# Last FFN of a hybrid encoder block: the last column group in two quads of seven block products, two weight sums of each by accumulating transfers

## Chip, cores and metric

The kernel runs on one core of one Trainium2 chip. The metric is device time in microseconds (us) of one execution; lower is better. A core has a tensor engine (PE; its weight loads are listed as PEld), a vector engine (DVE), a scalar engine (ACT), a GpSimd engine (POOL) and a sync engine (SP). In this kernel SP issues the plain weight loads, and POOL issues the few transfers that add to what lies in SBUF.

## What is computed

The reference is one residual block on `x` (256 tokens, width 2048): a SwiGLU feed-forward half step, a mixer of mLSTM heads and a gated linear recurrence, and a second SwiGLU half step. Only the last one matters here:

```python
def _swiglu(u, w13, w2):
    g, v = jnp.split(u @ w13, 2, axis=-1)
    return (jax.nn.silu(g) * v) @ w2
...
        y = _swiglu(modulate(x, 2), ffn2_w13[l], ffn2_w2[l])
        x = _layer_norm(ALPHA * x + FFN_WEIGHT * gate[:, 2, None, :] * y, ln_g[l, 2], ln_b[l, 2])
```

`w13` is 2048 x 11264 (gate half and value half of 5632 columns each), `w2` is 5632 x 2048, all in float32.

## The kernel before

**Precision.** The tensor engine multiplies in fp32r. Each float32 weight tile is split into a high part (a cast on ACT, name `h...`) and a low part (a subtraction raw minus high on DVE, name `l...`); activations are split in the same way. A product of a weight block (512 rows x 512 columns, one 1 MB tile of 128 x 2048) with 128 tokens is 12 matmuls of 128x512: for each of four row blocks high x high, low weight x high, high weight x low, in this order (`mov_t`). So the first matmul of a product needs the high part and the second needs the low part.

**Tiling of the last FFN (`last_ffn`, L1167).** The 5632 hidden columns go in 11 groups b = 0 to 10 of 512. A group needs eight weight tiles of `w13`, four row quarters of the gate columns (tiles 0 to 3) and four of the value columns (4 to 7), for two token halves t = 0, 1. Done plainly, that is 16 products. `fast_group` (L1361) does it with fewer. A *quad* q is the 2 x 2 x 2 problem made of two row quarters (2q, 2q+1), the gate and value columns, and the two token halves; with a = tile 2q, b = 2q+1, c = 4+2q, d = 5+2q it takes seven products in place of eight, each with its own weight tile:

- P1 uses a. P5 uses c - a, which DVE writes over a. P6 uses a - c - d, which DVE writes over the same place. P3 uses d, P2 uses b.
- P7 uses c + d, written over c; P4 uses a - c - d + b, written over a once more.

The two last sums are made either by DVE or, in the groups listed in `SUMMED` (L48), by a transfer that POOL issues and that adds the tile from HBM to what stands in SBUF (`onto`, L1219). The place a is thus written and read in a row: loaded, split for P1, summed, split for P5, summed, split for P6, summed, split for P4.

The first token sums that P5, P6, P3 and P7 multiply are in `ws[0]` (for quad 0) and `ws[1]` (for quad 1), made once.

**Single and double groups.** A single group has quad 0 in seven products and the other two row quarters in plain products: G (gate columns) and V (value columns), two tiles each, 24 matmuls a tile. A double group (listed in `DOUBLE`, L45) has both quads in seven products. Groups 2, 4, 6 and 8 are double, 1, 3, 5, 7, 9 and 10 are single. The order of the products on PE is written out by hand in a string for each kind (S2, S4, S10, D6, L56 to L59): P1 to P7, G and V are products, X is a tile of the second matrix `w2` (24 matmuls, for the group before), and t turns a finished group of hidden values (four 128x128 transposes).

**Order on the other engines.** All work of this stage is first recorded as steps (`Plan`, L95). PE's steps keep the order of the strings. The planner gives each step of DVE, ACT, POOL and SP a due time from PE's steps that need it, and by its own costs and the buffers that come free it settles the order on each engine and the buffer that each tile takes. Every engine's queue then runs strictly in that order, each instruction waiting for what it needs.

**After group 10.** `gated` (L1573) prepares two `w2` tiles into the space of the activations; seven `w2` tiles follow (`end_tile`), then the last column tile and the final layer norm.

**Names in the profile.** `rfw` is a raw `w13` tile, `hfw_100P` / `lfw_100P` the high and low parts of the products of group 10, quad 0 (`101P` quad 1), `100G`, `101V` and so on the plain ones, `f` the accumulators and partial sums of a group, `th`/`ht` the turned hidden values, `lw`/`hw` a `w2` tile, `tl` its accumulators, `yacc` the residual. Nearly all instructions of this stage carry L359, the helper that records them.

Of the kernel before, what the change touches and what calls it, by code (L numbers as in the profile page):

```python
# [41 lines left out]

SLOT = 2176

DOUBLE = (2, 4, 6, 8)  # L45
HOLD = ("slot", "row")
BY_DMA = ("P2", "P3")
SUMMED = (1, 2, 3, 4, 5, 6, 7, 8, 9)  # L48
TURNED = ()
SOONER = True  # L50
ANY = ("raw", "lo", "slot", "row", "hi")
# [3 lines left out]

S4 = "P1 t X t P5 X P6 P3 X P7 P2 G P4 G X V V"  # L56
S2 = "P1 t G t P5 G P6 P3 P7 V P2 P4 V"
S10 = "P1 t G t P5 X P6 P3 P2 P4 G X P7 V V"
D6 = "P1 t X t P5 P6 X P3 P7 X P2 P4 X P1 X P5 P6 X P3 P7 X P2 P4 X"  # L59


# [33 lines left out]
class Plan:  # L95
# [14 lines left out]
    def place(self, tag, make, ap=None):  # L110
        tags = (tag,) if isinstance(tag, str) else tag
        p = Place(tags, (lambda _: make()) if isinstance(tag, str) else make, ap)
        if ap is not None and tags:
            p.tag, p.asked = tags[0], True
            self.taken[p.tag] += 1
        return p
# [166 lines left out]
def block_kernel(ctx: ExitStack, tc: tile.TileContext, a: dict, out: bass.AP):  # L283
# [80 lines left out]
    V, A, G, T, Q = (Pinned(e) for e in (nc.vector, nc.scalar, nc.gpsimd, nc.tensor, nc.sync))  # L364
# [146 lines left out]
    def mov_t(ps, hl, acth, actl, k0, t, first, last, pe=nc.tensor, **kw):  # L511

        hi, lo = hl
        tk = slice(t * P, (t + 1) * P)
        for j in range(4):
            w = slice(j * 512, (j + 1) * 512)
            o = like(ps, hi)
            pe.matmul(o, acth[:, k0 + j, tk], cut(hi, w), start=first and j == 0, stop=False, **kw)  # L518
            pe.matmul(o, acth[:, k0 + j, tk], cut(lo, w), start=False, stop=False, **kw)  # L519
            end = pe.matmul(o, actl[:, k0 + j, tk], cut(hi, w), start=False, stop=last and j == 3, **kw)  # L520
        return end
# [30 lines left out]
    def rows(k):  # L552

        return lambda: [u2[:, i:i + 4].rearrange("p a w b -> p (a w b)") for i in (k, k + 4)]
# [612 lines left out]
    def last_ffn(s, w13, w2):  # L1167
        n_b = NFF // 4
        sts = new_stats(s)
        plan = Plan({"raw": 4, "hi": 3, "lo": 3, "row": 2, "slot": 6, "ps": 8, "u": 2, "gy": 2, "x": 1})  # L1170
# [29 lines left out]
        def bank_place(name):  # L1200
            return place("ps", lambda: bank(name))
# [4 lines left out]
        def load(src, name, to=None):  # L1206
            p = to or raw_place(name)
            op("Q", 0.4, lambda: Q.dma_start(p(), src), writes=[p], moves=1.0)
            return p

        def split(p, name, into=None, by=None):
            hi = into[0] if into else any_place("h" + name, F32R, HIGH)
            lo = into[1] if into else any_place("l" + name, F32R, LOW)
            op("A", 1.82, lambda: A.copy(hi(), like(p(), hi())), reads=[p], writes=[hi], seq=None if into else "hi", by=by)
            op("V", 2.21, lambda: V.tensor_sub(lo(), like(p(), lo()), hi().bitcast(F32)), reads=[p, hi],
               writes=[lo], seq=None if into else "lo", by=by)
            return hi, lo
# [7 lines left out]
        def pe(n, fn, reads, writes):  # L1225
            op("T", n * 0.2268, fn, reads=reads, writes=writes)

        def tokens_of(k0, t):
            return [("u", k0 // 4, t)]

        def hl_of(hl):
            return hl[0](), hl[1]()
# [128 lines left out]
        def fast_group(b, quads, xs, steps, then={}):  # L1361

            i = 8 * b
            single = quads == 1
            by_dma = BY_DMA if b in SUMMED else ()
            W, f, ps, seen, done, made = {}, {}, {}, {}, {}, set()
# [1 line left out]
            u = uh, ul  # L1368

            def part(key, hl, h, k0, t, first, last, again=False):  # L1370
                if first and key not in ps or (key == "1" and first):
                    ps[key] = bank_place(f"f{key}{b}")
                p = ps[key]
                act = (lambda: u) if h is u else (lambda: hl_of(h))
                pe(12, lambda: mov_t(p(), hl_of(hl), *act(), k0, t, first, last, T, skip_group_check=again),
                   [*hl, *(tokens_of(k0, t) if h is u else h)], [p])

            def normal(key, hl, h, k0, t):
                seen[key] = n = seen.get(key, 0) + 1
                part(key, hl, h, k0, t, n == 1, n == uses[key])  # L1380
# [129 lines left out]
        def gate_row():  # L1510
            ps, row = bank_place(f"adag{s}"), place(None, lambda: sm.tile([KT, P], F32, tag="grow", bufs=1, name=f"grow{s}"))
            gate2 = any_place("gate2", F32, HOLD)

            def spread():
                gate.tile = gate2()
                G.dma_start(gate2(), rowd.rearrange("a b -> (a b)").rearrange("(o n) -> o n", o=1).to_broadcast([P, D]))

            op("T", 0.2, lambda: T.transpose(ps()[0:KT, 0:P], adac[:, s, 2, :], ident), reads=[("adac", k) for k in range(KT)], writes=[ps])
            op("A", 0.3, lambda: A.mul(row(), ps()[0:KT, 0:P], 0.5), reads=[ps], writes=[row], by=4.0)
            op("G", 0.6, lambda: G.dma_start(rowd, row()), reads=[row], writes=["rowd"], moves=0.3)  # L1520
            op("G", 0.6, spread, reads=["rowd"], writes=[gate2], moves=0.5)
            return gate2
# [10 lines left out]
        for b in range(2, n_b - 1, 2):  # L1533
            kgs = (b - 2, b - 1)
            xs = x_tiles(kgs, range(4))
            if b == n_b - 3:
                gate2 = gate_row()
            if b in DOUBLE:
                if len(ws) == 1:
# [17 lines left out]
        pss, hls = {}, {}  # L1557
# [15 lines left out]
        def gated(k, by):  # L1573
            p = load(w2[kgs[k] * 4 + 3], f"w2{s}l{k}")
            for c in range(0, D, 512):
                op("V", 0.62, lambda c=c: V.tensor_mul(p()[:, c:c + 512], p()[:, c:c + 512], gate2()[:, 1536:]),
                   reads=[p, gate2], writes=[p])
            into = [place(None, lambda w=w: rows(8 * (k - 1))()[w]) for w in range(2)]
            for h in into:
                h.also = [("u", 2 * (k - 1) + i, t) for i in range(2) for t in range(NT)]  # L1580
            hls[k] = [h() for h in split(p, "", into, by - plan.now)]

        def first_tiles():
            for k in range(2):
                end_tile(0, k)
                yield

        fast_group(n_b - 1, 1, first_tiles(), S10, {"P4": lambda: gated(1, plan.now + 14.0)})
        gated(2, plan.now + 20.0)
        for i, (n, k) in enumerate(((1, 0), (1, 1), (2, 0), (0, 2), (1, 2), (2, 1), (2, 2))):  # L1590
            end_tile(n, k)
# [389 lines left out]
    softplus_lambda()  # L1981
    mixer((a["w13_2"][0:8], "f", (0, 1), (1,), (), True, 6))
    last_ffn(2, a["w13_2"], a["w2_2"])


# [89 lines left out]
```

## Time and profile before

| what | value |
|---|---|
| three runs | 1860.46, 1861.64, 1862.16 us (median 1861.64) |
| the profiled execution's own time | 1859.48 us |
| its span, first to last instruction | 1857.7 us |
| busy in the span: PE, PEld, DVE, ACT, POOL | 1842.9, 1511.5, 1610.5, 932.0, 66.2 us |
| group 10 on PE | from 1739.06 us, its last product ends near 1791.8 us |

All durations below come from the one profiled execution, whose time is 2.16 us under the median of the three runs; its span leaves 1.78 us of its time outside. In a timeline row the first number is the start from the span's beginning, the second the time of the (merged) instructions, and the bracket the engine's idle time just before with what ended it. In the chain of waits, each piece is what stood on the path to the end, with its start and length. Consecutive instructions of one engine overlap a little in these rows, so the distance between two starts, not the duration, says how fast they follow.

### The profile page before, as it was taken

The page shows a single profiled execution, that of the slowest core. Times are in us where ns is not written, and L with a number is a line of the kernel's source. Part 1 is how long each engine was busy: PE and PEld are TensorE (multiplying, and loading weights), DVE is VectorE, ACT ScalarE, POOL GpSimd, SP SyncE. Part 2 cuts the span into 40 slices and gives each one's busy share as a digit, 9 for nine tenths or more (in the row PEclk, how much of TensorE's full clock was granted, in tenths as well). Part 3 has the DMA queues.
Part 4 walks back from the last instruction along what each step waited for, and adds up shares of the span by engine and source line. Part 5 has one row for each costly group of instructions (what it writes and reads, how often), then busy time and mean ns, then how long its engine had stood idle before and what let it go on. Part 6 is the DMA issues. An engine that isn't in the chain of part 4 may idle for free.

```text
span 1857.7 us, 21314 instructions
## 1 busy us (share of the span) xinstructions
PE 1842.9 (99%) x8423; PEld 1511.5 (81%) x8423; DVE 1610.5 (87%) x1506; ACT 932.0 (50%) x874; POOL 66.2 (4%) x94
## 2 busy tenths in 40 slices
PE   8999999999999999999999999999999999999998
PEld 5788888888888888788888887888888888888886
DVE  6899998888887986889997778899999989989886
ACT  4533444534333335564844346766565655665550
POOL 0000000000000000100000021000000000000000
PEclk9999999999999999999999999999999999999999
DMA  9999889999999897368678654888988888888852
GB/s 376 416 363 355 323 317 345 349 345 354 348 366 362 336 345 271 157 259 287 264 281 310 239 207 191 317 287 249 316 298 279 312 247 312 277 255 280 276 226 91
DMA packets 78677, 547.34 MB, mean 295 GB/s; under 512 B 9153, under 2 KB 9329, under 8 KB 13937
## 3 DMA queue, kind: packets, MB, share of 16 engines
q1 hardware_dynamic: 72144, 507.54, 71.2%
q0 software_dynamic: 4704, 34.63, 9.1%
q10 hardware_dynamic: 1728, 3.80, 0.6%
q8 instruction: 66, 1.08, 0.2%
q14 instruction: 35, 0.28, 0.0%
HBM read 541.72 MB, written 4.22 MB: 294 GB/s over the span
## 4 chain that ended last, share of the span: by engine, by line
PE 93%; DVE 3%; DMA 1%; ACT 1%; issue 1%; POOL 0%; POOLq 0%; DVEq 0%; SPq 0%; ACTq 0%
PE f L359 23%; PE py L359 9%; PE pj L507 6%; PE tl L359 4%; PE py L519 3%; PE py L520 3%; PE py L518 3%; PE pj L509 3%; PE fg L519 2%; PE fg L520 2%; PE fg L518 2%; PE fv L519 2%; PE fv L518 2%; PE fv L520 2%; PE rv L982 2%; PE rv L983 2%
## 5 line engine op out<-in xcount | busy, mean ns | idle before, releaser
L436 DVE CUSTOM_DVE_ANT_0 ada<-ada,scb,badac 128x2048 f32<-128x2048 f32 x94 | 220.4, 2345 | 21.3 <-DMA ada<-in_w_ada 21.1
L359 PE MATMUL py<-hw,ht 128*128 128x512 f32 x512 | 163.2, 390 | 0.0
L332 ACT CAST hra<-rra 128x2048 fp32r<-128x2048 f32 x38 | 72.6, 1915 | 102.2 <-DMA rra<-in_w_r 35.0
L332 ACT CAST hw<-rw 128x2048 fp32r<-128x2048 f32 x40 | 76.6, 1914 | 91.7 <-DMA rw<-in_w 46.9
L507 PE MATMUL pj<-u,hs 128*128 128x512 f32 x512 | 122.5, 391 | 0.0
L359 DVE CUSTOM_DVE_ANT_0 ada<-ada,scb,badac 128x2048 f32<-128x2048 f32 (+1 forms) x50 | 110.8, 2217 | 4.2 <-DMA ada<-in_w_ada 4.0
L359 PEld LDWEIGHTS py<-hw,ht 128*128 128x128 f32 x512 | 96.1, 188 | 19.8
L334 DVE TENSOR_TENSOR lw<-rw,hw 128x2048 fp32r<-128x2048 f32 x40 | 91.3, 2287 | 23.0 <-ACT hw L332 23.0
L507 PEld LDWEIGHTS pj<-u,hs 128*128 128x128 f32 x512 | 94.3, 188 | 18.4
L359 PE MATMUL py<-lw,ht 128*128 128x512 f32 x256 | 99.7, 389 | 0.7 <-DVE lw L359 0.7
L519 PE MATMUL py<-lw,hth 128*128 128x512 f32 x256 | 99.8, 390 | 0.1
L520 PE MATMUL py<-hw,htl 128*128 128x512 f32 x256 | 99.7, 390 | 0.0
L518 PE MATMUL py<-hw,hth 128*128 128x512 f32 x256 | 97.3, 392 | 0.0
L359 DVE TENSOR_TENSOR lw<-rw,hw 128x2048 fp32r<-128x2048 f32 x41 | 93.6, 2287 | 4.2 <-PE py L359 1.9
L332 ACT CAST hs<-rs 128x2048 fp32r<-128x2048 f32 x32 | 61.0, 1909 | 68.8 <-PE pj L507 63.6
L359 ACT CAST hw<-rw 128x2048 fp32r<-128x2048 f32 x41 | 78.4, 1911 | 32.8 <-DMA rw<-in_w 12.9
L334 DVE TENSOR_TENSOR ls<-rs,hs 128x2048 fp32r<-128x2048 f32 x32 | 73.0, 2280 | 11.4 <-ACT hs L332 11.4
L359 DVE TENSOR_TENSOR lra<-rra,hra 128x2048 fp32r<-128x2048 f32 x29 | 66.3, 2286 | 8.9 <-ACT hra L359 6.8
L509 PEld LDWEIGHTS pj<-u,ls 128*128 128x128 f32 x512 | 65.6, 191 | 2.5
L332 ACT CAST hfg<-rfg 128x2048 fp32r<-128x2048 f32 x20 | 38.3, 1916 | 57.6 <-DMA rfg<-in_w 57.6
L509 PE MATMUL pj<-u,ls 128*128 128x256 f32 x512 | 66.4, 283 | 0.0
L334 DVE TENSOR_TENSOR lfv<-rfv,hfv 128x2048 fp32r<-128x2048 f32 x20 | 45.8, 2290 | 21.2 <-ACT hfv L332 21.0
(794 smaller groups left out, 5023.2 us busy)
## 6 DMA issues: line engine op xcount, KB each, us to landing
ada<-in_w_ada SPq DMA_DIRECT2D x138, 1024.0 KB, 6.8
rw<-in_w SPq DMA_DIRECT2D x81, 1024.0 KB, 6.9
rfw<-in_w SPq DMA_DIRECT2D x56, 1024.0 KB, 7.2
rra<-in_w_r SPq DMA_DIRECT2D x45, 1024.0 KB, 7.5
rs<-in_w_s SPq DMA_DIRECT2D x32, 1024.0 KB, 5.1
rfw<-in_w POOLq DMA_DIRECT2D x26, 1024.0 KB, 9.2
rfv<-in_w SPq DMA_DIRECT2D x23, 1024.0 KB, 6.7
rfg<-in_w SPq DMA_DIRECT2D x20, 1024.0 KB, 6.4
```

Source lines behind the costliest of these rows:

```text
L332: act.copy(cut(hi, w), like(raw[:, w], hi))
L334: low.tensor_sub(cut(lo, w), like(raw[:, w], lo), cut(hi, w).bitcast(F32))
L359: self.last = getattr(self.engine, op)(*args, **kw)
L436: vec.tensor_tensor_reduce(raw[:, c], raw[:, c], scb[:, c], 1.0, base, ALU.mult, ALU.add, to)
L507: nc.tensor.matmul(ps, hi[:, k * P:(k + 1) * P], both(k), start=k == 0, stop=False)
L509: nc.tensor.matmul(ps[:, 0:S], lo[:, k * P:(k + 1) * P], uh[:, k, :], start=False, stop=k == KT - 1)
L518: pe.matmul(o, acth[:, k0 + j, tk], cut(hi, w), start=first and j == 0, stop=False, **kw)
L519: pe.matmul(o, acth[:, k0 + j, tk], cut(lo, w), start=False, stop=False, **kw)
L520: end = pe.matmul(o, actl[:, k0 + j, tk], cut(hi, w), start=False, stop=last and j == 3, **kw)
L982: pe.matmul(pss[t], uh[:, k0 + j, tk], hi[:, w], start=go, stop=False)
L983: pe.matmul(pss[t], uh[:, k0 + j, tk], lo[:, w], start=False, stop=False)
```

## The change

Group 10 becomes a double group, its two quads' sums c + d and a - c - d + b go by accumulating transfers, and the order string S10 is rewritten:

```diff
-DOUBLE = (2, 4, 6, 8)
+DOUBLE = (2, 4, 6, 8, 10)
...
-SUMMED = (1, 2, 3, 4, 5, 6, 7, 8, 9)
+SUMMED = (1, 2, 3, 4, 5, 6, 7, 8, 9, 10)
...
-S10 = "P1 t G t P5 X P6 P3 P2 P4 G X P7 V V"
+S10 = "P1 t P5 t P6 P3 P7 P2 P4 P1 X P5 P6 X P3 P7 P2 P4"
...
-                if first and key not in ps or (key == "1" and first):
+                if first and (key not in ps or key == "1"):
...
-        fast_group(n_b - 1, 1, first_tiles(), S10, {"P4": lambda: gated(1, plan.now + 14.0)})
+        fast_group(n_b - 1, 2 if n_b - 1 in DOUBLE else 1, first_tiles(), S10, {"P4": lambda: 1 in hls or gated(1, plan.now + 14.0)})
```

The line on `ps` is the same condition in other words. The last line lets the second P4 pass without preparing the gated tile again.

Over the whole program PE gets 7354 matmuls of 128x512 instead of 7366, DVE 7 more instructions (two 128x2048 tensor-tensor, one 128x2048 scalar-tensor-tensor, four 128x512 adds), ACT three more 128x2048 casts, POOL four more transfers, SP the same number. `ws[1]`, two tiles of 128x2048, stays in its places until P7 of the second quad; before, it was last read in group 8.

**DVE at the first quad of group 10.** Names here carry buffer numbers: `rfw2_100` is the place a of quad 0, `rfw2_104` c, `rfw2_105` d, `rfw2_101` b; `lfw2_100P5` is the low part for P5; `f129`, `f329`, `f529` are partial sums of group 9, `lw22_8_0` the low part of the first `w2` tile. Before:

```order
L359 TENSOR_TENSOR f129_12069<-f129_12069,f29_12056 128x512
L359 TENSOR_TENSOR rfw2_100_12172<-rfw2_104_12213,rfw2_100_12172 128x2048
L359 TENSOR_TENSOR f329_12229<-f329_12229,f49_12077 128x512
L359 TENSOR_TENSOR yacc1_9114<-yacc1_9114,gate2_11540 128x512
L359 TENSOR_TENSOR f229_12190<-f229_12190,f59_12103 128x512
L359 TENSOR_TENSOR f129_12069<-f129_12069,f229_12190 128x512
L359 TENSOR_TENSOR f529_12135<-f529_12135,f19_12031 128x512
L359 TENSOR_TENSOR lfw2_100P5_12337<-rfw2_100_12172,hfw2_100P5_12302 128x2048
L359 TENSOR_TENSOR f329_12229<-f329_12229,f529_12135 128x512
L359 TENSOR_TENSOR lw22_8_0_12360<-rw22_8_0_12266,hw22_8_0_12318 128x2048
L359 SCALAR_TENSOR_TENSOR rfw2_100_12172<-rfw2_100_12172,rfw2_105_12268 128x2048
```

The same place now:

```order
L359 TENSOR_TENSOR f129_12070<-f129_12070,f29_12057 128x512
L359 TENSOR_TENSOR lfw2_91V_12275<-rfw2_91V_12189,hfw2_91V_12258 128x2048
L359 TENSOR_TENSOR lfw2_100P1_12280<-rfw2_100_12153,hfw2_100P1_12273 128x2048
L359 TENSOR_TENSOR rfw2_100_12153<-rfw2_104_12191,rfw2_100_12153 128x2048
L359 TENSOR_TENSOR f329_12224<-f329_12224,f49_12077 128x512
L359 TENSOR_TENSOR f229_12187<-f229_12187,f59_12099 128x512
L359 TENSOR_TENSOR f129_12070<-f129_12070,f229_12187 128x512
L359 TENSOR_TENSOR lfw2_100P5_12327<-rfw2_100_12153,hfw2_100P5_12308 128x2048
L359 SCALAR_TENSOR_TENSOR rfw2_100_12153<-rfw2_100_12153,rfw2_105_12226 128x2048
L359 TENSOR_TENSOR f529_12135<-f529_12135,f19_12031 128x512
L359 TENSOR_TENSOR f329_12224<-f329_12224,f529_12135 128x512
L359 TENSOR_TENSOR ht9_12350<-th90_12329,ht9_12350 128x4x128
```

The next row is the low part for P6. The low parts of 91V and of P1, which stood ahead of the first add before, now stand behind it; the low parts of P5 and P6 follow at once.

**DVE at the end of the first quad and in the second.** `rfw2_102` is place a of quad 1; `rw22l1` is the gated `w2` tile. Before:

```order
L359 TENSOR_TENSOR lfw2_100P4_12457<-rfw2_100_12172,hfw2_100P4_12453 128x2048
L359 TENSOR_TENSOR ht9_12376<-th90_12339,ht9_12376 128x4x128
L359 TENSOR_TENSOR lfw2_101G_12490<-rfw2_101G_12335,hfw2_101G_12475 128x2048
L359 TENSOR_TENSOR lw22_9_0_12496<-rw22_9_0_12431,hw22_9_0_12492 128x2048
L359 TENSOR_TENSOR ht9_12376<-th91_12381,ht9_12376 128x4x128
L359 TENSOR_TENSOR rw22l1_12455<-rw22l1_12455,gate2_11540 128x512 x3
```

The same place now:

```order
L359 TENSOR_TENSOR lfw2_100P4_12441<-rfw2_100_12153,hfw2_100P4_12424 128x2048
L359 TENSOR_TENSOR lfw2_101P1_12447<-rfw2_102_12277,hfw2_101P1_12439 128x2048
L359 TENSOR_TENSOR rfw2_102_12277<-rfw2_106_12385,rfw2_102_12277 128x2048
L359 TENSOR_TENSOR lw22_8_0_12480<-rw22_8_0_12404,hw22_8_0_12464 128x2048
L359 TENSOR_TENSOR lfw2_101P5_12485<-rfw2_102_12277,hfw2_101P5_12482 128x2048
L359 SCALAR_TENSOR_TENSOR rfw2_102_12277<-rfw2_102_12277,rfw2_107_12422 128x2048
L359 TENSOR_TENSOR f1210_12348<-f1210_12348,f110_12467 128x512
L359 TENSOR_TENSOR rw22l1_12443<-rw22l1_12443,gate2_11540 128x512 x3
L359 TENSOR_TENSOR lfw2_101P6_12534<-rfw2_102_12277,hfw2_101P6_12515 128x2048
L359 TENSOR_TENSOR rw22l1_12443<-rw22l1_12443,gate2_11540 128x512
L359 TENSOR_TENSOR lw22_9_0_12555<-rw22_9_0_12462,hw22_9_0_12538 128x2048
```

The second quad's sums and splits take the place of the plain tiles' splits, and the two `w2` splits stand between them.

**POOL from the last accumulating transfer of group 9.** Before:

```order
L359 DMA rfw2_90_11904<-in_w13_2 128x2048
L359 DMA yacc0_9108<-xd_121 128x2048
L359 DMA yacc1_9114<-xd_121 128x2048
L359 TENSOR_SCALAR vep20_13010<-mvp20_13008 128x1
L359 TENSOR_TENSOR rsp20_13012<-vep20_13010,mhalf_78 128x1
```

The same place now:

```order
L359 DMA rfw2_90_11904<-in_w13_2 128x2048
L359 DMA yacc0_9108<-xd_121 128x2048
L359 DMA yacc1_9114<-xd_121 128x2048
L359 DMA rfw2_104_12191<-in_w13_2 128x2048
L359 DMA rfw2_100_12153<-in_w13_2 128x2048
L359 DMA rfw2_106_12385<-in_w13_2 128x2048
L359 DMA rfw2_102_12277<-in_w13_2 128x2048
L359 TENSOR_SCALAR vep20_13020<-mvp20_13018 128x1
```

Four adding transfers of group 10 stand behind the two that add the residual into `yacc`.

## Prediction

> **What bounds the kernel now.** First the waits of PE over the last 550 us, which hold nearly all of the last FFN (engine, tile, what it waited for: us in total, times, longest):
>
> ```profile
> PE tz L359 <- ACT dm L359: 0.8, 1, 0.8
> PE py L359 <- DVE lw L359: 0.7, 1, 0.7
> ```
>
> PE waits twice in 550 us, once for the final norm and once, 0.7 us, for a low half from DVE. So PE's own work sets the end there, and it is the low halves that come closest to stopping it. The chain of waits says the same about group 10 (start, us, what):
>
> ```profile
> 1706.56 35.39 PE f L359 x156
> 1741.95 0.44 PE th L359 x4
> 1742.38 5.47 PE f L359 x24
> 1747.86 0.44 PE th L359 x4
> 1748.29 2.75 PE f L359 x12
> 1751.04 5.44 PE tl L359 x24
> 1756.48 16.32 PE f L359 x72
> ```
>
> Only PE stands there. 35.39 us for 156 matmuls is 0.227 us each: a product of 12 costs 2.72 us, a plain or `w2` tile of 24 5.44, a turn 0.44. Next the windows (length, then busy of PE, PEld, DVE, ACT, POOL, then granted clock, DMA share, GB/s), one of them from the start of group 10 over the next 64 us:
>
> ```profile
> 25.00:40.00 15.00, 13.08 (x31) 5.62 (x30) 7.71 (x11) 4.64 (x8) 0.00 (x0) 1.00 1.03 418
> 1700.00:1739.00 39.00, 39.00 (x177) 32.33 (x176) 35.20 (x24) 26.60 (x20) 2.56 (x3) 1.00 0.90 278
> 1739.00:1803.00 64.00, 64.00 (x289) 52.95 (x289) 57.95 (x39) 38.31 (x26) 0.00 (x0) 1.00 0.65 240
> 1848.00:1858.00 10.00, 2.88 (x7) 0.74 (x5) 5.04 (x8) 0.60 (x2) 1.69 (x2) 0.87 0.33 109
> ```
>
> PE is busy throughout, but DVE is busy 57.95 us of 64: 6.05 us from being the bound itself. The durations that I use are in these DVE, ACT, PE and POOL rows, and in the page's list of transfers (KB each, median us to landing):
>
> ```profile
> 1704.23 2.29 DVE L359 TENSOR_TENSOR lfw_91G<-rfw_91G,hfw_91G 128x2048 fp32r<-128x2048 f32 x1
> 1706.44 6.69 DVE L359 TENSOR_TENSOR lfw_90P<-rfw,hfw_90P 128x2048 fp32r<-128x2048 f32 x3
> 1731.10 0.69 DVE L359 TENSOR_TENSOR f<-f,f 128x512 f32<-128x512 f32 x1 [0.37 <-PE f L359]
> 1744.88 2.28 DVE L359 SCALAR_TENSOR_TENSOR rfw<-rfw,rfw 128x2048 f32<-128x2048 f32 x1
> 1766.86 1.88 DVE L359 TENSOR_TENSOR rw22l<-rw22l,gate 128x512 f32<-128x512 f32 x3
> 1747.19 3.73 ACT L359 CAST hfw_100P<-rfw 128x2048 fp32r<-128x2048 f32 x2 [1.61 <-DVE rfw L359]
> 1756.34 1.92 ACT L359 CAST hfw_100P<-rfw 128x2048 fp32r<-128x2048 f32 x1 [2.37 <-PE tl L359]
> 1739.06 0.39 PE L359 MATMUL f<-hfw_100P,u 128*128 128x512 f32 x1
> rfw<-in_w SPq DMA_DIRECT2D x56, 1024.0 KB, 7.2
> rfw<-in_w POOLq DMA_DIRECT2D x26, 1024.0 KB, 9.2
> ```
>
> A 128x2048 DVE operation starts 2.20 us after the one before it (1704.23 to 1706.44; three in 6.69) and its result is there after 2.29; a 128x512 one takes 0.60 in a row (three in 1.88). A cast on ACT takes 1.92. The last two rows compare a plain load (7.2) with an adding transfer (9.2).
>
> **What goes.** Twelve matmuls: 12 x 0.227 = 2.72 us off PE, all on the path. That is 0.15% of 1859.48; 0.2%, about what a measurement can tell from no change, is 3.7 us. So even if nothing waits the gain stays under what can be told.
>
> **What comes on the vector engines.** DVE gets three more 128x2048 operations and four more 128x512: 3 x 2.20 + 4 x 0.60 = 9.0 us; ACT three casts, 5.8 us. ACT has 25.7 us idle in that window, so its sum is nothing by itself. DVE has 6.05 us, and PE would want the window 2.72 us shorter. Much of the new work can't be pulled ahead, as the order shows: the low parts of 91V, of P1 and all that follows stand behind `f129`, whose other operand is the product P2 of group 9. In the row above DVE waits for just that until 1731.10. So I walk the queues from there.
>
> **The first quad.** DVE in the new order: `f129` 1731.10, 91V 1731.7, P1 1733.9, the sum for P5 1736.1 to 1738.4, three adds to 1740.1. ACT casts P5 from 1738.4 to 1740.3; DVE splits it 1740.3 to 1742.6, makes P6's sum 1742.5 to 1744.8; ACT casts 1744.8 to 1746.7 (DVE's three small operations fit behind that); DVE splits 1746.7 to 1749.0. PE: P1 from 1739.06, as the PE row has it, turn, P5 at 1742.2 whose second matmul (the low part) wants 1742.45 and gets 1742.6: 0.15 late. Turn, P6 could start at 1745.5; its high part comes at 1746.7, 1.2 late, its low part at 1749.0 against 1746.95, 2.05 late more. Before, P6 came 17.4 us after P1 with a G and an X between; now it comes 6.4 us after. **P6: 3.25 late.**
>
> Then the sum for P4 is added on the place a, which P6's split must have read: POOL issues it at 1749.0. The transfer's time is not in the trace for this place; the nearest rows are the adding transfers of the other groups and the two that add the residual (min, median, max of issue to landing; the first line is theirs alone, of 26, the second of the two):
>
> ```profile
> DMA to landing us min/median/max: 7.9/9.2/14.0
> DMA to landing us min/median/max: 9.4/10.9/12.4
> ```
>
> P4's casts and split take 1.92 + 2.29 = 4.2. PE meanwhile has the rest of P6 (to 1751.5), P3, P7, P2: P4 could start at 1759.7 and wants its low part at 1759.95. With 9.2 the high part comes at 1760.1, the low at 1762.4: 2.45 late in all; with 7.9 1.2, with 14.0 7.3. Five plain loads are issued beside it, as beside the two of `yacc`, so I take 10.0, between the medians 9.2 and 10.9: **P4: 3.25 late.** Behind it on POOL stand the two sums of quad 1; `rfw_106`'s goes only after that quad's own P5 sum, so this queue costs nothing more. P7's sum is issued at 1738.4 and P7 due at 1754.2: even 14.0 leaves it no later than 1752.4 plus a 1.92 cast, just in time.
>
> **The second quad.** Here it is DVE alone. Call 0 the end of P4's split. Low of P1 is done at 2.3, P5's sum at 4.4, low of the first `w2` tile at 6.7; PE ends P4 at 2.5, P1 at 5.2, and wants the low part at 5.45: 1.25 late. P5's split follows, P6's sum ends at 11.1, four small operations to 13.4, P6's split at 15.7; PE (the rest of the `w2` tile 5.2, P5 2.72) wants it at 14.85: 0.85 late. The second `w2` tile's split is 0.05 late; after that three products of one split each go by in 2.72 to 2.20, and the next `w2` tile is again about 0.3 late, with four small adds ahead of it. **1.25 + 0.85 + 0.35 = 2.45 late.**
>
> Check by the whole window: 57.95 + 9.0 = 67.0 us of DVE work against 61.3 us of PE work, 5.7 late at least if nothing is moved out of it; the walk gives more since DVE also waits for ACT and for the transfer.
>
> **What stays.** From the first `w2` tile of column tile 1 on, order and work are those of before, with PE as the bound, and the end of the program (from the last column tile on) keeps its length.
>
> **Sum.** 0.15 + 3.25 + 3.25 + 2.45 = 9.1 late, less 2.72: +6.4. On the profiled execution that is 1859.48 + 6.4 = 1865.9; its time is 2.16 under the median of the three runs, so on the median 1861.64 + 6.4 = **1868.0**. With the transfer at 7.9 it is +4.3 (1866.0), at 14.0 +10.4 (1872.1).
>
> **Rivals.**
>
> *A: not slower, the splits run ahead.* The four double groups have the same chain of sums and PE never waits in them (the two waits above are all). If DVE and the loads come early enough that the lateness stays under 2.72 us in all, the matmuls win: at best -2.72, 1858.9, which is within 0.2%. It decides at whether `f129` really holds the queue at 1731.1. Against it: in D6 an X of 5.44 us stands between P1 and P5 and two between P6 and P4 (21.8 us from P6 to P4; here 10.9 in quad 0), so their slack is not here. 0.06.
>
> *B: the adding transfer is hidden.* If it lands within 6.7 us of its issue, P4 is on time and the sum is 0.15 + 3.25 + 2.45 - 2.72 = +3.1, 1864.8, still within 0.2%. The Trainium skill, "DMA: Bandwidth & Descriptors", section "Anatomy of one DMA", fits a transfer issued by GpSimd as 2.0 us plus its bytes at 436 GB/s; an estimate from it for 1 MB is 4.4 us, by which P4 would not wait and B would be the outcome. The trace disagrees: 26 of 26 took 7.9 or more here. 0.05.
>
> *C: a load is late already ahead of P1.* `ws[1]` keeps two places that loads used before, so 91V's load goes out behind a's of group 10, and the two `yacc` transfers overlap it. In the trace before the second load of quad 0 went out as in the first row, and the load of 101G, beside the `yacc` transfers, took as long as the second row says:
>
> ```profile
> 1717.27 0.33 SPq L359 DMA_DIRECT2D rfw_100G<-in_w  x1
> ```
>
> ```profile
> DMA to landing us min/median/max: 15.0/15.0/15.0
> ```
>
> A load of 91V issued at about 1717.3 then lands at 1732.3; cast, 1734.2: 2.5 after DVE's turn at 1731.7, and everything behind it moves with it. +8.9, 1870.5. 0.17.
>
> *D: the clock.* In the windows above 1.92 us of idle PE between 25 and 40 left the clock at 1.00; it fell only at the end, with PE idle for over 7 us. P6's wait of 1.2 and 2.05 with one matmul between comes nearer than any wait before. Should the rest of P6, 2.5 us, run at half speed, that is +2.5: +8.9, 1870.5. The Trainium skill, "TensorE: Matmul & The Clock Gate", section "What's actually happening", lets the clock halve after an idle window of about 3.4 us; by that rule 3.25 us in two pieces is just not enough, and the trace has no wait between 1.92 and the end to test it. 0.07.
>
> That the change doesn't do what it says is excluded by the matmul count.
>
> **How the numbers follow.** Forecast 0.63, C 0.17, D 0.07, A 0.06, B 0.05, the rest unknown. Slower by over 0.2%: 0.63 + 0.17 + 0.07 and the unknown's half, 0.88; within 0.2%: A and B, 0.10; faster by over 0.2%: 0.02, since no step here can give it. The range takes in the forecast's own 1866.0 to 1872.1 and C and D, and on the low side goes to B's 1864.8 almost: 1864.8 to 1872.5.
>
> **What would show it.** In the profile after: PE waits for DVE at P6 and P4 of 100P (about 3 us each) and at the first `tl` (about 1.3), and for ACT at the high parts just ahead of the first two; DVE near 100% from 1736 to 1800; the first adding transfer on place a issued near 1749 and landing 9 to 11 us later; the chain of waits passing through DVE and a transfer between 1738 and 1785. The reading is wrong if PE has no waits there, if `f129` starts well ahead of 1731, or if the loss lies after the first `w2` tile of column tile 1.

## The result, and the profile after

The changed kernel takes 1872.26 us (median of four runs, 1871.98 to 1874.62) against 1861.18 us for the kernel before on the same chip: 1.0060 times as long, 95% interval 1.0048 to 1.0072, that is 11.1 us more (8.9 to 13.4). On another chip it took 1870.60 against 1860.87, ratio 1.0054 (1.0041 to 1.0066). The forecast was 6.4 us more, with a range to 1872.5.

The waits of PE from 1700 to 1815 in the profile after (engine, tile, what it waited for: us in total, times, longest):

```profile
PE f L359 <- DVE lfw_100P L359: 3.7, 2, 1.8
PE f L359 <- DVE lfw_91V L359: 1.8, 1, 1.8
PE f L359 <- ACT hfw_91V L359: 1.7, 1, 1.7
PE tl L359 <- DVE lw L359: 1.5, 2, 1.2
PE f L359 <- DVE lfw_101P L359: 0.7, 1, 0.7
PE f L359 <- ACT hfw_100P L359: 0.3, 1, 0.3
```

The first row holds one wait at P6 and one at P4 of quad 0, the last row is P4's high part, and the `tl` and `lfw_101P` rows are the second quad: all three places stand in the forecast. The wait for ACT at P6's high part, forecast at 1.2 us, did not come. The two rows on 91V were not in the sum: 91V is the last V tile of group 9, directly ahead of group 10 on PE. The chain of waits names what was late there (start, us, what):

```profile
1707.36 10.71 PE f L359 x48
1718.07 16.21 DMA rfw_91V<-in_w
1734.36 1.91 ACT hfw_91V L359
1736.29 2.30 DVE lfw_91V L359
1738.63 10.80 PE f L359 x35
...
1750.99 1.81 ACT hfw_100P L359
1752.82 2.30 DVE lfw_100P L359
1755.41 8.65 DMA rfw<-in_w
1764.45 1.92 ACT hfw_100P L359
1766.39 2.30 DVE lfw_100P L359
...
1816.34 43.57 PE tl L359 x192
```

A plain load of 16.21 us, issued at 1718.07, is on the path. Before, the same load was issued 7 us earlier, took 8.5 us and stood on no path:

```profile
L359 SPq DMA_DIRECT2D rfw_91V<-in_w x1: 328/328/328, 1711.0 to 1711.0; - x1
...
DMA to landing us min/median/max: 8.5/8.5/8.5
```

Behind it come P6's cast and split, the adding transfer on place a, and P4's cast and split, in the order that the forecast walked. The last row is the column tiles at the end, 12.7 us later than in the chain before and of the same length. There it was:

```profile
1803.62 43.57 PE tl L359 x192
```

The windows (length, then busy of PE, PEld, DVE, ACT, POOL, granted clock, DMA share, GB/s):

```profile
1700.00:1739.00 39.00, 35.45 (x159) 28.87 (x158) 27.91 (x19) 21.12 (x17) 2.62 (x4) 0.98 0.88 234
1739.00:1803.00 64.00, 58.20 (x244) 46.33 (x244) 58.23 (x39) 36.90 (x25) 3.44 (x4) 0.96 0.85 262
1737.00:1744.00 7.00, 5.37 (x13) 4.21 (x14) 6.94 (x5) 2.39 (x3) 0.36 (x1) 0.52 1.01 425
```

PE lost 3.55 us of the first window, which held no wait before, and 5.80 of the second. In the third its clock stood at half, behind the two waits for 91V. DVE was busy 58.23 of the 64 us, 91%, and not near 100% as forecast: it too waited, 3.69 us for 91V's high part and 3.30 us for P4's. The rows of PE themselves, with the idle time ahead of each in the bracket:

```profile
1736.31 0.49 PE L359 MATMUL f<-hfw_91V,u 128*128 128x512 f32 x1 [1.72 <-ACT hfw_91V L359]
1738.63 0.80 PE L359 MATMUL f<-lfw_91V,u 128*128 128x512 f32 x1 [1.83 <-DVE lfw_91V L359]
...
1755.17 0.50 PE L359 MATMUL f<-lfw_100P,ws 128*128 128x512 f32 x1 [1.83 <-DVE lfw_100P L359]
...
1766.41 0.49 PE L359 MATMUL f<-hfw_100P,u 128*128 128x512 f32 x1 [0.30 <-ACT hfw_100P L359]
1768.74 0.50 PE L359 MATMUL f<-lfw_100P,u 128*128 128x512 f32 x1 [1.83 <-DVE lfw_100P L359]
...
1775.65 0.50 PE L359 MATMUL tl<-lw,ht 128*128 128x512 f32 x1 [1.18 <-DVE lw L359]
...
1784.78 0.50 PE L359 MATMUL f<-lfw_101P,ws1h 128*128 128x512 f32 x1 [0.66 <-DVE lfw_101P L359]
...
1804.49 0.50 PE L359 MATMUL tl<-lw,ht 128*128 128x512 f32 x1 [0.30 <-DVE lw L359]
```

A bracket undercounts what a wait costs: idle time is counted from the modelled end of the matmul before (0.39 or 0.49 after its start), while the next would have started after 0.227. So each wait costs its bracket plus 0.16 or 0.27: 1.88 and 2.10 at 91V, 2.10 at P6, 0.46 and 2.10 at P4, 1.33, 0.81 and 0.46 in the second quad. The halved clock adds 2.7: 13 matmuls from 1738.63 to 1744.26, 5.63 us, where 13 x 0.227 = 2.95 is due. All these terms are from one execution.

### The profile page after: what moved, and what is told of

It is laid out like the page before. It is cut to its first block, busy times and chain, and to the rows that moved or that the text cites. A ratio compares the mean times of both kernels' runs of the same rounds, so it can differ in the third digit from the quotient of the medians.

```text
span 1870.5 us, 21329 instructions
## 1 busy us (share of the span) xinstructions
PE 1845.7 (99%) x8411; PEld 1511.3 (81%) x8411; DVE 1619.8 (87%) x1513; ACT 936.9 (50%) x877; POOL 67.6 (4%) x98
## 4 chain that ended last, share of the span: by engine, by line
PE 86%; DVE 5%; DMA 4%; issue 3%; ACT 2%; POOL 0%; POOLq 0%; DVEq 0%; SPq 0%; ACTq 0%
PE f L359 18%; PE py L359 8%; PE pj L507 5%; PE tl L359 4%; PE py L519 3%; PE py L520 3%; PE py L518 3%; PE pj L509 3%; PE fg L519 2%; PE fg L520 2%; PE fv L519 2%; PE fg L518 2%; PE fv L518 2%; PE fv L520 2%; PE rv L982 2%
```

## Experiments

**Theory 1.** Three things are late. (i) 91V's load goes out 7 us later than before (1718.07 against 1710.95), presumably because `ws[1]` keeps two places, and it lands beside three adding transfers; DVE's queue stands behind it. (ii) In quad 0 the chain of sums and splits from P1 to P4 is longer than the products on PE that cover it. (iii) In the second quad DVE is the bound. **Theory 2.** DVE has 67 us of work against 61 of PE, and nothing else matters. **Theory 3.** The later issue alone explains 91V. In the diffs below, + is the experiment, and ratios are to the kernel before on the same chip.

### Where the two residual transfers go

`held_residual`:

```diff
-        for t in range(NT):
+        def residual_in(t):
...
+                s.before.add(plan.seq["T"])
+                plan.seq["T"].after.add(s)
...
+        AT = [('P6', 1), ('P1', 2)]
```

`s` is each product of `yacc` with the gate, which thus waits for PE's last recorded step; `AT` names the products of group 10 behind which the two halves are recorded.

> The changed kernel, but the two residual transfers into yacc, and the products of yacc with the gate ahead of them on DVE, are recorded at P6 of the first quad and P1 of the second instead of ahead of group 10; on POOL they now stand behind the four adding transfers of group 10. Theory 1 (91V's load comes late because it lands beside three adding transfers, 16.2 us, and DVE's queue stands 4.6 us behind it; ACT then holds P6's cast a further 1.1 us behind PE, whose clock was halved): 91V lands within 10 us, DVE starts its split by 1732.5, P6's split 5 to 6 us earlier than now, and the kernel takes about 5.7 us less, 1866.5 (1865 to 1868). Theory 2 (DVE has 67 us of work against 61 of PE, and when the residual comes plays no part): 1872, no change. Theory 3 (the two places that ws[1] keeps delay the loads by themselves): 91V is issued as late as now and is as late at ACT, 1872.

`no_residual`:

```diff
-            op("G", 0.6, lambda y=y, t=t: G.dma_start(y(), xd[:, t, :], accum_op=ALU.add), reads=["xd"],
-               writes=[(y, n) for n in range(4)], moves=1.8)
```

> The changed kernel without the two residual transfers into yacc, so that the residual is missing from the output; all else stands in the order of the changed kernel, the products with the gate too. It takes away two of the three adding transfers beside which 91V lands, and nothing from PE, ACT or DVE. Theory 1: 91V is issued at 1718 as now but lands by 1728, ahead of DVE's turn at 1731.9; about 5.7 us less, 1866.5 (1865 to 1868). Theory 2: 1872. Theory 3 (places, so issue times alone): 91V lands as late as now, 1872.

Measured: `held_residual` 1866.61, ratio 1.0033 (1.0021 to 1.0044), `no_residual` 1863.98, ratio 1.0019 (1.0010 to 1.0027). Against the changed kernel's 1.0060 these are 5.0 and 7.6 us less (against its second measurement, 1.0054, 3.9 and 6.5). The loads of 91V in the profile of `held_residual`, then in that of `no_residual` (issue, then time to landing):

```profile
L359 SPq DMA_DIRECT2D rfw_91V<-in_w x1: 327/327/327, 1715.6 to 1715.6; - x1
...
DMA to landing us min/median/max: 10.8/10.8/10.8
```

```profile
L359 SPq DMA_DIRECT2D rfw_91V<-in_w x1: 328/328/328, 1718.7 to 1718.7; - x1
...
DMA to landing us min/median/max: 8.0/8.0/8.0
```

In `no_residual` 91V leaves as late as in the changed kernel and lands in half the time, and PE no longer waits for it. So theory 3 falls, and theory 2 cannot say where 5 to 7 us went with the same work on DVE. What stays in `no_residual` is 3.4 us over the kernel before (1863.98 against 1860.55). That is near the least that the forecast's check by the whole window allows, 5.7 - 2.72 = 3.0, but no run shows that DVE's total work sets it. A caution: the planner reordered a few small DVE steps in both kernels too; the splits of 91V start at 1730.28 and 1729.60, earlier than the 1731.7 of the forecast's walk, and in both PE then waits at the turn of group 9's hidden values (`th`) for DVE, 2.3 us in `held_residual` and 1.4 in two pieces in `no_residual`.

The converse, `early_residual`, on the kernel before:

```diff
-                   writes=[(y, n)])
+                   writes=[(y, n)], by=-16.0)
```

> The kernel before with the products of yacc with the gate asked for 16 us earlier, so that all eight stand in a row on DVE between the low halves of 90V and of P2 of group 9, and the two residual transfers go out near 1717 and 1721 as in the changed kernel; one quad, ws[1] not kept. Theory 1 (the loss at 91V has two causes that are both needed: it is issued 7 us later because ws[1] keeps two places, and it lands beside three adding transfers): 91V goes out at about 1711 to 1714, lands 12 to 16 later, by 1728, ahead of its turn, and PE does not wait for it; other loads may be 0 to 2 us late: 1860.5 to 1862.5. Rival (the early residual transfers cost their 5 us whatever the issue times): 1865 to 1867.

Measured: 1861.64, ratio 1.0004 (0.9995 to 1.0013), so no loss that can be told. The residual transfers go out at 1717.5 and 1718.7 and take 13.0 and 19.2 us, the load of 100G beside them 14.5 us. But 91V had left at 1711.4 and was there after 8.5, and in the last FFN PE's only new wait is 0.2 us. Both are needed: a load that leaves late, and company that doubles its time. Why it leaves late is not shown as clearly: 91V's load goes out at 1711.0 to 1713.8 in the four profiles with one quad and at 1714.5 to 1719.8 in the ten with two, but no run keeps the two places of `ws[1]` and changes nothing else.

### What an adding transfer costs

`no_a_sum` (P4 of quad 0 multiplies what P6's sum left):

```diff
-                        onto(a, w13[i + 2 * q + 1])
+                        if (b, q) != (10, 0):
+                            onto(a, w13[i + 2 * q + 1])
```

> The changed kernel without the adding transfer on place a of the first quad (1755.41 to 1764.06, 8.65 us), so that P4 of that quad multiplies what P6's sum left there and the output lacks that part. P4's cast can then follow those of P3, P7 and P2, and nothing else changes. Theory 1 (the P4 step of the forecast: P4 of the first quad waits 2.56 us in two pieces, and it waits for the transfer): both waits at P4 go, DVE loses 3.3 us of idle time there, and the time falls by 2.6 to 3.3: 1869.3. Rival (DVE's queue is so late by then that its own work takes the place of the transfer at once): the wait at P4 or at the next low part stays, less than 1 us gained, 1871.5.

Measured: 1869.75, ratio 1.0046 (1.0033 to 1.0058): 2.6 us less than 1.0060, 1.5 less than 1.0054. P4 has no wait left in the profile, so the P4 term is the transfer's. Its size is shown only roughly, since the interval overlaps with those of the changed kernel.

`one_sum`, on the kernel before:

```diff
-SUMMED = (1, 2, 3, 4, 5, 6, 7, 8, 9)
+SUMMED = (1, 2, 3, 4, 5, 6, 7, 8, 9, 10)
```

> The kernel before (group 10 with one quad and its G and V tiles) with the sums for P7 and P4 made by adding transfers instead of DVE: half of the change alone. DVE loses 2 x 2.20 = 4.4 us in group 10. In the kernel before, P6's low part is done at 1753.7 and P4 starts at 1764.64; the sum on place a goes out at about 1753.7, lands 9.2 later (7.9 to 10.9), and cast and split take 4.2. Theory 1 (the transfer and not DVE sets P4): P4's low part is there at 1767.1 against 1764.87, 2.2 late (0.9 to 3.9): 1862.8 on the chip on which the kernel before takes 1860.55. Rival (DVE's total work is what counts, so 4.4 us less of it can only help): 1860.5 or less.

Measured: 1872.12, ratio 1.0059 (1.0047 to 1.0072). Half of the change alone costs as much as the whole, 11 us, and my 2.2 was far off. P4 waits 8.6 us by the brackets, and behind that PE's clock stood at 0.50 from 1772 to 1782. The two waits at P4, and the landing of the transfer on place a, issued at 1754.4:

```profile
1774.50 0.79 PE L359 MATMUL f<-hfw_100P,u 128*128 128x512 f32 x1 [7.03 <-ACT hfw_100P L359]
1776.83 0.79 PE L359 MATMUL f<-lfw_100P,u 128*128 128x512 f32 x1 [1.53 <-DVE lfw_100P L359]
```

```profile
L359 POOL DMA_DIRECT2D rfw<-in_w x1: 859/859/859, 1754.4 to 1754.4; - x1
...
DMA to landing us min/median/max: 18.1/18.1/18.1
```

It took 18.1 us where I had taken 9.2 (7.9 to 10.9). The second residual transfer had gone out 2.2 us ahead of it, at 1752.2. That this company is the cause is what `one_sum_held` tries: `one_sum` with the residual recorded behind group 10.

> The kernel before with the two sums of group 10 made by adding transfers (as in the run one_sum, where the transfer on place a took 18.09 us beside the second residual transfer, 12.89 us), but with the two residual transfers recorded behind group 10, so that they go out after it. Theory 1 (an adding transfer takes 8 to 9 us alone and 12 to 18 beside another one): the transfer on place a lands in 8 to 10 us, P4 waits 1 to 3 us in all where it waited 9.2, the clock stays up, and the time is 1861.5 to 1863.5 on a chip on which the kernel before takes 1860.6. Rival (P4 follows P6 too closely for a transfer of any length, or plain loads alone slow it): 1868 to 1872.

Measured: 1861.28, ratio 1.0004 (0.9995 to 1.0012). The same transfer, issued at 1754.1:

```profile
DMA to landing us min/median/max: 8.8/8.8/8.8
```

PE waits nowhere in group 10. From the same place and 0.3 us apart in time, the adding transfer of 1 MB took 8.8 us without another one beside it and 18.1 with one, and that goes with some 10 us of the kernel's time (1.0059 against 1.0004). One difference stays beside it: while the transfer was out, or up to 4 us ahead of it, `one_sum` issued four plain loads and `one_sum_held` three. The lower end of my expectation, 1861.5, was still too high.

### DVE's queue

`dve_sums`, on the changed kernel, so that all four sums of group 10 are DVE's:

```diff
-SUMMED = (1, 2, 3, 4, 5, 6, 7, 8, 9, 10)
+SUMMED = (1, 2, 3, 4, 5, 6, 7, 8, 9)
```

> The changed kernel with the sums for P7 and P4 of both quads of group 10 made on DVE instead of by four adding transfers. DVE gets 4 x 2.20 = 8.8 us more. Theory 1 (from 1736 to 1800 it is the queue of DVE that sets the time, and the wait at P4 of the first quad, 2.56 us, is the transfer's): the wait for the transfer goes, -2.6, and 8.8 us come on DVE's queue of which that wait (3.3 us of idle DVE) takes some: 2 to 6 us more, 1874 to 1878. Rival (the transfers are what costs, DVE still has room in its idle time of 5.8 us in 64): 1868 to 1872.

Measured: 1881.62, ratio 1.0112 (1.0096 to 1.0127), 9.7 us over the changed kernel, where 2 to 6 were expected. From 1736 to 1786, the changed kernel and then `dve_sums`:

```profile
1736.00:1786.00 50.00, 42.06 (x170) 32.95 (x171) 44.28 (x29) 26.64 (x21) 3.44 (x4) 0.93 0.85 268
```

```profile
1736.00:1786.00 50.00, 35.74 (x142) 28.16 (x143) 47.65 (x30) 25.44 (x20) 0.00 (x0) 0.87 0.45 178
```

DVE is idle 2.35 us of 50 in `dve_sums` against 5.72, so the 3.3 us in which it waited for the transfer did take some of the new work, as I had thought. PE loses 6.3 more all the same. Its longest wait is a new one, 7.6 us inside the first `w2` tile, for turned hidden values (`ht`) that stand on DVE's queue behind the second quad's splits until 1784.57, and its clock was 0.87 against 0.93. So more work on DVE costs time, but the size here is also that of the order which the planner chose.

`x_first` moves the two X of group 10 into the first quad:

```diff
-S10 = "P1 t P5 t P6 P3 P7 P2 P4 P1 X P5 P6 X P3 P7 P2 P4"
+S10 = "P1 t X t P5 P6 X P3 P7 P2 P4 P1 P5 P6 P3 P7 P2 P4"
```

> The changed kernel with its two X (w2 tiles of column tile 0) moved from the second quad into the first: one between P1 and P5, one between P6 and P3, as in the four other double groups. Theory 1 (the chain of P6 and P4 is too short in the first quad, but behind it DVE alone is the bound, with 67 us of work against 61 of PE): the waits at P6 and P4 of the first quad go, and since the second quad then has only 12-matmul products against DVE's 2.2 to 4.4 us for each, waits of about the same sum come at its P5, P6 and P4: 1870 to 1874. Rival (the loss at P6 and P4, 5 us, is a matter of the order alone): 1867.

Measured: 1875.95, ratio 1.0076 (1.0063 to 1.0088). Its waits from 1739 to 1815:

```profile
PE f L359 <- DVE lfw_101P L359: 5.6, 3, 2.0
PE tl L359 <- DVE lw L359: 2.2, 1, 2.2
PE f L359 <- ACT hfw_101P L359: 2.0, 2, 1.5
...
```

No row on `100P` is left: the first quad runs through, and the second waits instead, for 5.6 + 2.0 us at its own P products. The order moves the waits and doesn't remove them; the total came out above the 1870 to 1874 expected. Nobody waits for 91V here: its load goes out at 1714.5, takes 11.2 us beside the same three adding transfers, and PE runs through to 1739. But DVE then sits idle 3.72 us, until 1736.14, for the high part of P1, the next tile, whose own load ACT had waited for until 1734.20. So the waits for 91V are not a sum that can simply be taken off: late loads that stop DVE come back at the next place where PE needs it.

`no_q1_sum`:

```diff
-                        sum_of(a, a, c, lambda o: V.tensor_sub(o, c(), o))
+                        if (b, q) != (10, 1):
+                            sum_of(a, a, c, lambda o: V.tensor_sub(o, c(), o))
```

> The changed kernel without the sum for P5 of the second quad (2.20 us on DVE; P5 of that quad multiplies a itself, and the output is another one). Theory 1 (the second quad is bound by DVE, lateness 1.33 at the first tl, 0.81 at P6, 0.46 at the second tl in the profile after): everything behind the sum moves up by 2.2 us on DVE, the three pieces shrink to 0 to 0.4 in all, 2.2 to 2.6 less: 1869.8. Rival (these waits are set by loads or by ACT): within 0.5 of 1872.

Measured: 1873.22, ratio 1.0063 (1.0049 to 1.0077): no gain in the time, against 2.2 to 2.6 expected. In the profile, its rows at P4's low part and at the last wait of the group:

```profile
1769.20 0.50 PE L359 MATMUL f<-lfw_100P,u 128*128 128x512 f32 x1 [1.83 <-DVE lfw_100P L359]
...
1783.76 0.50 PE L359 MATMUL f<-lfw_101P,ws1h 128*128 128x512 f32 x1 [0.66 <-DVE lfw_101P L359]
1803.83 0.50 PE L359 MATMUL tl<-lw,ht 128*128 128x512 f32 x1 [0.51 <-DVE lw L359]
```

From the first to the last of them it takes 34.63 us where the changed kernel takes 1804.49 - 1768.74 = 35.75. The first `tl` wait is gone, the other two stay: 1.1 us gained there, half of what was expected, since the splits behind waited for PE and ACT for part of the 2.2 us. A new wait of 1.3 us for the last column tile's low part (`lol`) gives it back. So for the second quad the size is only bounded: DVE's queue sets at least the first of its three waits.

### The clock

`warm`:

```diff
                 elif w == "V":
+                    if (b, q) == (9, 1):
+                        z = bank_place("warm")
+                        pe(8, ...)   # eight matmuls of u by u into z
```

> The changed kernel with eight extra matmuls of 128x512 (1.8 us) on PE just ahead of the second V tile of group 9 (91V), on a bank that nothing reads, so that the first of the two waits for 91V (1.88 us) is filled with work. The clock should then not fall, since the waits of 2.1 us later on leave it at full speed. Theory 1a (the halved clock delays PE by 2.65 us, but DVE's chain does not wait for PE there; it only reaches P6 through ACT, whose copy of P1's sum holds P6's cast by 1.1 us): 1.1 us less, 1871.2. Theory 1b (the clock's 2.65 us lie on the path as a whole): 2.65 less, 1869.6. If the clock falls nevertheless: no change, or up to 0.5 more.

`after_again`:

> The changed kernel as it is, for its time on the chip of the three runs beside it. All theories: 1.0060 times the kernel before, about 1871.8 where that takes 1860.6; the profile with 91V landing 15 to 16.5 us after its issue and the same waits.

Measured: `warm` 1870.35, ratio 1.0052 (1.0040 to 1.0065), `after_again` 1870.60, 1.0054 (1.0041 to 1.0066). Between them there is no difference to see. Against 1.0060 `warm` would be 1.5 us less, with overlapping intervals, so neither 1b's 2.65 us nor 1a's 1.1 us is shown. In the profile of `warm` the filler did its work: the clock stood at 1.00 from 1737 to 1749; it fell at P6's wait instead (0.79 from 1750 to 1756). The profile of `after_again` says why the filler has little to win. Here are its waits for 91V and at the start of P6, then its windows:

```profile
1735.72 0.51 PE L359 MATMUL f<-hfw_91V,u 128*128 128x512 f32 x1 [1.69 <-ACT hfw_91V L359]
1738.04 0.50 PE L359 MATMUL f<-lfw_91V,u 128*128 128x512 f32 x1 [1.82 <-DVE lfw_91V L359]
...
1750.71 0.63 PE L359 MATMUL th<-ident,f 128*128 128x128 f32 x4 [1.02 <-DVE f L359]
1753.48 0.79 PE L359 MATMUL f<-lfw_100P,ws 128*128 128x512 f32 x1 [1.82 <-DVE lfw_100P L359]
```

```profile
1738.00:1744.00 6.00, 5.96 (x26) 4.96 (x27) 5.86 (x5) 1.40 (x1) 0.86 (x1) 1.00 1.00 425
1753.00:1757.00 4.00, 3.52 (x9) 2.80 (x10) 2.63 (x2) 3.50 (x2) 0.86 (x1) 0.57 0.47 63
```

The same two waits of the same kernel left the clock at 1.00 this time. PE then came to P6 earlier and waited 1.2 us longer ahead of it, at the turn, for DVE. The clock fell there instead. So this pair can't tell what the halved clock at 91V costs: in the profile without the filler it had not fallen there either.

`held_warm`, on `held_residual`:

```diff
                 elif w == "P4":
+                    if (b, q) == (10, 0):
+                        z = bank_place("warm")
+                        pe(12, ...)   # twelve matmuls of u by u into z
                     normal("4", hl, u, ku + 4, 1)
```

> The run held_residual with twelve extra matmuls of 128x512 (2.72 us) on PE just ahead of P4 of the first quad, on a bank that nothing reads, to fill its first wait (2.82 us); there the waits of 2.82 and 2.10 us with one matmul between halved the clock for 6.8 us in the profiled execution, of 1869.02, while others took 1865.6 to 1865.9. Theory 1 (the executions differ by that halved clock, and DVE is not the bound right behind it, so that up to 2.65 us of it lie on the path): the clock stays up behind P4, all executions lie near 1865.7, the median 1 to 2 us under the 1866.6 of held_residual at equal time of the kernel before. Rival (the loss is taken up by the waits behind, or the remaining wait halves the clock all the same): no change, 1866.6.

Measured: 1868.12, ratio 1.0041 (1.0028 to 1.0053), not better than `held_residual` at 1.0033, so theory 1 fails here. The clock behind P4 did stay up, but it fell at another wait. The same stretch of `held_residual` and then of `held_warm`, around a wait of 2.29 us at the turn ahead of P5 that both have at 1744.4:

```profile
1741.00:1744.00 3.00, 1.12 (x5) 0.58 (x4) 2.97 (x3) 0.16 (x1) 0.00 (x0) 1.00 1.05 218
1744.00:1748.00 4.00, 3.60 (x20) 3.04 (x20) 3.86 (x5) 4.00 (x4) 0.00 (x0) 1.00 0.80 285
```

```profile
1741.00:1744.00 3.00, 1.12 (x5) 0.58 (x4) 2.97 (x3) 0.16 (x1) 0.00 (x0) 1.00 1.03 213
1744.00:1748.00 4.00, 3.59 (x11) 3.02 (x12) 3.87 (x5) 4.00 (x3) 0.00 (x0) 0.57 0.80 281
```

Busy times agree to 0.02 us, and only one of the two lost its clock. None of the variants with two quads came under the kernel before. The best of those that compute the whole reference is `held_residual`.

## Why the prediction was right in direction and short in size

**The sign, the places and the mechanism held.** The forecast named P6 and P4 of quad 0 and the start of the second quad, with DVE's queue and one adding transfer as what ends last; all stand in the waits and in the chain. Slower by over 0.2% had 0.88, and 1872.26 lies just inside the upper end of the range, 0.24 us from it, an end that was set for rivals C and D and not by the sum. The signs that were to show the reading came in part: the transfer on place a went out at 1755.41 and not near 1749, and landed after 8.65 us and not 9 to 11.

**Where the 12.8 us of the span (1857.7 to 1870.5) are,** beside the forecast's terms:

| term | forecast | measured |
|---|---|---|
| twelve matmuls less | -2.72 | -2.72 (taken over, not seen by itself) |
| wait for 91V | 0 | 3.98 |
| clock at half behind it | 0 | 2.7 |
| P5, second matmul | 0.15 | 0.1 |
| P6 | 3.25 | 2.10 |
| P4 | 3.25 | 2.56 |
| second quad | 2.45 | 2.60 |
| PE already later before this stage (1707.36 against 1706.56) | 0 | 0.8 |
| what is left over, among it slower first steps behind each wait | 0 | 0.7 |

The 0.8 us are there long before this stage: one step on PE starts at 1615.60 in the profile after and at 1614.80 before; their cause is open. The forecast's own terms came to 7.4 of 9.1. **The step that failed is the start of the walk:** "91V 1731.7", that is, that DVE would find 91V's high part ready. It waited 3.69 us for it and started that split at 1736.29. Rival C had just this, "91V's load goes out behind a's of group 10, and the two `yacc` transfers overlap it", at 0.17. It priced the landing at 1732.3 and the time at 1870.5; the load went out 0.8 later and took 1.2 longer, landing at 1734.28, and C's price with these 2.0 us is 1872.5, against 1872.26. So the outcome was C in its mechanism. That the price comes so near is partly luck: C has nothing for the 2.7 us of the clock and the 0.8 us at the start, and P6 and P4 measured 1.8 us less than in its sum. Its issue time was partly luck as well: the row at 1717.27 is the load of 100G, a plain gate tile, and not the second load of quad 0, as the forecast says. What was mis-sized was its chance. In the profile after, the last four products of `yacc` with the gate stand close together on DVE, two ahead of and two behind the low half of 90V, where before they stood in four places as far down as group 10; of this the order lists ahead of the forecast already showed that a product of `yacc1` had left the first quad of group 10. The residual transfers went out at 1717.35 and 1721.33, before at 1725.73 and 1735.49. And it was plain that `ws[1]` still held its places. Either alone leaves 91V in time (`early_residual`, `no_residual`). Since this change brings both, they come together, and 0.17 was too little.

**P6.** It measured less than forecast only because PE came late itself. DVE's queue was 4.6 us behind the walk at 91V and 5.0 at the end of P6's sum (1749.75 against 1744.8), and ACT held P6's cast another 1.1 (it began at 1750.87, behind a copy that waited for PE), while PE could start P6 7.3 late (1752.84 against 1745.5): 3.25 + 5.0 + 1.1 - 7.3 = 2.05, against 2.10. With 91V in time a loss of that size stands one place earlier, as 2.3 us at the turn (`held_residual`, 1744.4).

**P4.** The transfer was taken as 10.0 and took 8.65; with the forecast's own scale from 9.2 (2.45) to 7.9 (1.2) that makes 1.9, and 2.56 was measured. `no_a_sum` gives 1.5 to 2.6 back. Rival B, which wanted it within 6.7, fell: the four adding transfers of group 10 took 7.9 to 9.6 us.

```profile
DMA to landing us min/median/max: 7.9/8.3/9.6
```

The Trainium skill, "DMA: Bandwidth & Descriptors", section "Anatomy of one DMA", by whose fit I had estimated 4.4 us for 1 MB, is off by a factor of two here for adding transfers that go by themselves, and by four for the one of `one_sum`.

**The second quad.** 2.60 against 2.45, in three pieces (1.33, 0.81, 0.46) against three (1.25, 0.85, 0.35). The sum agrees; that DVE alone is the reason is shown for the first piece only.

**Rival D, the clock,** came too, in the profiled execution at 91V and not at P6. Its 2.7 us are in the table of that execution, but in that of `after_again` the clock held there, and PE reached P6 earlier and waited for DVE instead. It is no term that can be added.

**With 91V in time** the sum comes near: `held_residual`, with 91V's split at 1730.28, is 6.1 us over the kernel before (1866.61 against 1860.55), where the forecast had +6.4. Term by term it is the forecast only in part. The transfer on place a goes out at 1748.4, as forecast, and takes 11.3 us; P4 waits 2.66 and 1.83 us by the brackets, 4.9 with what they undercount, where the forecast's scale gives about 4.6 for such a transfer. But the loss at P6 stands at the turn, and behind P4 the clock stood at 0.50 from 1764 to 1769, a term that the sum put at nothing. So the near agreement of the totals is partly luck too.

## What to carry to other kernels

Replacing a vector operation by a transfer that adds in place is free only if its landing, with everything that is in flight beside it, still leaves the cast and the split their time: list the other adding transfers that will be out at the same moment, not only the one that you add. When a change makes a buffer live longer and lets other transfers go earlier, follow the one load that leaves last ahead of the new work. A load that comes late costs most where the engine behind it has little idle time left, and then mending one wait can move the loss to the next (`x_first`). Rivals that share a cause with the change (here places kept and transfers moved up) deserve more than the chance that each has by itself.

## What the runs showed of the hardware that I had not expected

- **Adding transfers slow each other and the plain loads beside them.** Where two of 1 MB went out within 4 us of each other, the second took 13.2 (`held_warm`), 16.7 (the changed kernel), 18.1 (`one_sum`) and 19.2 us (`early_residual`). Without another adding one in flight they took 7.8 to 12.4 from group 9 on, and the 26 of the kernel before 7.9 to 14.0 with a median of 9.2, so the two ranges meet, and something else, plain loads perhaps, can stretch one as well. In the changed kernel's group 10 it was 7.9 to 9.6, in `one_sum_held` 8.8. The two of the residual in the changed kernel overlap each other and one of group 9:

```profile
DMA to landing us min/median/max: 13.3/15.0/16.7
```

  The plain load of 91V beside these three took 16.2 us; without the two, issued 0.6 us later and with the plain loads around it in the same order, 8.0.
- **Whether a wait halves the clock can't be read from its length.** Waits of 1.88 and 2.10 us with one matmul between halved it in one execution and not in the next of the same kernel, and the single wait of 2.29 us in one of two kernels that are alike up to there. The Trainium skill, "TensorE: Matmul & The Clock Gate", section "What's actually happening", says that the activity window of about 3.4 us runs freely and is not tied to the kernel. That the outcome varies from execution to execution agrees with that; the windows themselves are not in the trace. But the same section lets the clock halve after an idle window of that length, and here it fell behind a single wait of 2.29 us (`held_warm`), so a shorter wait can be enough.
